# A written order for the first stages of a two-layer diffusion block on one core

## The chip, the cores and the metric

The kernel runs on one core of a Trainium2 chip. The metric is the device time of one execution in microseconds; lower is better. The core has five instruction streams that matter here: TensorE (PE, with its weight loads as PEld), VectorE (DVE), ScalarE (ACT), GpSimd (POOL) and SyncE (SP). Transfers from memory are issued from the streams of SP, ACT or POOL and carried by 16 DMA engines.

## The reference

Two layers of a transformer-like block work on 256 context tokens and 256 latent tokens of width 1024, in float32. Each layer has a token mixer (differential attention, a gated linear recurrence called HGRN, windowed attention, merged by gates) and a squared-ReLU MLP. What the change touches is the very beginning: the vectors that modulate the input, the norm of the input, and the first input projections.

```python
c_act, cc_act = silu(c), silu(c_ctx)
for l in range(DEPTH):
    m_l = split((c_act  @ w_ada[l] + b_ada[l]), 6)      # shift, scale, gate, ... latent
    m_c = split((cc_act @ w_ada[l] + b_ada[l]), 6)      # the same for the context
    h_l = rms_norm(x,   norm_g[l, 0]) * (1 + m_l[1]) + m_l[0]
    h_c = rms_norm(ctx, norm_g[l, 0]) * (1 + m_c[1]) + m_c[0]
    ... [h @ w for w in split_columns(w_in[l])] ...      # all mixers' projections
```

So the first projection needs w_ada's columns for shift and scale (1024 rows of 2048 columns) before anything can be multiplied with w_in.

## The kernel before

Float32 products are made of three matmuls on halves: a value is split into a rounded high part (`hi`, written by a ScalarE copy) and the rest (`lo`, a VectorE subtraction), and `hi*hi`, `hi*lo`, `lo*hi` are added up in PSUM (lines 248 to 250, and 260 to 262 where the activations are the stationary operand). A weight block of 1024 by 256 is loaded in two halves of 512 KB into `raw` and split into `whl` (lines 217, 226, 227); two blocks fit `whl`, a third one `arr`.

The instructions are traced in program order, and a scheduler then puts them in order on each engine by a simulation of the whole program; `high_priority` moves a piece up, and `issue_after(i)` makes an instruction stand behind `i` in its engine's queue without a wait. Temporary buffers come from an arena (`arf`, 33 units of 512 columns), the least recently freed unit first, so a load can wait for the last reader of the unit it is given. The framework gives the loads of SP's and ScalarE's queues eight semaphores in turn: one of them is issued when the load eight before it has landed.

`setup` (line 262) loads the four token tiles of 512 KB, the identity (`cst`, 64 KB), and c, c_ctx, norm_g, hgrn_lb and b_ada into two units, `ra` and `rb`. Two transposes on TensorE (lines 284, 287) make columns of them (`prm`, `bT`), and silu(c) becomes `CA`. `first_norm` normalises each token tile and transposes it (line 485) into `xT`; each 128x128 piece is copied from PSUM by itself (lines 489, 491).

`first_blocks` (line 512) then works in four groups q of 256 channels:

- sums: eight loads of w_ada, 256 KB each, as four runs of 128 columns per row, and 32 small matmuls on them (line 535, bank b7);
- vectors: the sums are copied out (line 433), transposed (line 437), and become shift and scale (lines 443, 466);
- modulation of two channel tiles of 128, k = q and 4 + q (lines 504, 506), then `hi` by ScalarE (508) and `lo` by VectorE or, for even k, GpSimd (510);
- three pieces of w_in, 256 KB each (two gate blocks and the query block of the first two HGRN heads), loaded and split (lines 546, 547).

The products with the three blocks (i = 0, 1, 2; two column halves u; banks b0 to b5; 36 matmuls of 512 columns per group, 144 in all) are traced after all four groups. Behind the last group each bank is read by a sigmoid (lines 689, 698), and the HGRN heads start on VectorE and GpSimd (lines 765, 766). `setup_mixers` then loads ten constants of the mixers (1064 KB, lines 301 to 308) on SP's queue and prepares them. The next blocks (`tm_pair`, line 260, and so on) follow.

```python
            for k in range(8):
                raw = self.A.get(1)
                load(raw[:, :].rearrange("p (j c) -> p j c", j=4),
                     wa[k * 128:k * 128 + 128, 0:2048].rearrange("p (j c) -> p j c", j=4)[:, :, qc])
```

Of the kernel before, what the change touches and what calls it, by code (L numbers as in the profile page):

```python
# [111 lines left out]
class Net:  # L112
# [152 lines left out]
    def setup(self):  # L265
# [9 lines left out]
        nc.sync.dma_start(ra[72:80, 0:128], I["c_ctx"].rearrange("(k p) -> k p", p=128))  # L275
        nc.sync.dma_start(ra[0:64, 0:128], I["norm_g"].rearrange("l i (k p) -> (l i k) p", p=128))
        nc.sync.dma_start(ra[80:96, 0:128], I["hgrn_lb"].rearrange("l r (k p) -> (l r k) p", p=128))
        nc.sync.dma_start(rb[0:96, 0:128], I["b_ada"].rearrange("l (k p) -> (l k) p", p=128))
# [19 lines left out]
    def setup_mixers(self):  # L298
        nc, A, I = self.nc, self.A, self.I
        with self.tc.issue_after(self.last_dma.ins):  # L300
            nc.sync.dma_start(self.msk, I["msk"])
            nc.sync.dma_start(self.cst[:, 128:C_END], I["cst"][:, 128:C_END])
            lv = A.get(1)
            for l in range(DEPTH):
                nc.sync.dma_start(self.sl[:, l * 128:l * 128 + 128], dram(I["diff_subln"], l * 128, [(0, 128), (1, 128)]))
                nc.sync.dma_start(self.hn[:, l * 128:l * 128 + 128], dram(I["hgrn_norm"], l * 128, [(0, 128), (1, 128)]))
                nc.sync.dma_start(self.snk[:, l * 8:l * 8 + 8], dram(I["swa_sink"], l * 8, [(0, 128), (1, 8)]))
                nc.sync.dma_start(lv[:, l * 256:l * 256 + 256], dram(I["diff_lambda"], l * 256, [(0, 128), (1, 256)]))
# [119 lines left out]
    def ada_done(self, l, g, qs=range(4), p2=None):  # L428
        nc = self.nc
        t = self.A.get(1)  # L430
        q0, nq = qs[0], len(qs)
        c = slice(q0 * 128, (q0 + nq) * 128)
        nc.vector.tensor_copy(t[:, c], self.ps[7][:, c])
        if p2 is None:
            p2 = self.mps()
        for q in qs:
            nc.tensor.transpose(p2[:, q * 128:q * 128 + 128], t[:, q * 128:q * 128 + 128], self.ident)
        t.free()
        out = self.M[l].rearrange("p (s g j q) -> p s g j q", s=2, g=3, j=4)[:, :, g]
        bb = self.bT[:, l * 48 + g * 16:l * 48 + g * 16 + 16].rearrange("p (j q) -> p j q", j=4)  # L440
        for s in range(2):
            src = view(p2, q0 * 128 + s, [(32, 4), (128, nq)])
            nc.vector.tensor_tensor(out=out[:, s, :, q0:q0 + nq], in0=src, in1=bb[:, :, q0:q0 + nq], op=ALU.add)
# [6 lines left out]
    def rstd(self, ms, cols, add=True):  # L450
# [4 lines left out]
        self.nc.gpsimd.tensor_tensor(out=r, in0=ms, in1=self.nhalf[:, 0:cols], op=ALU.pow)  # L455
        return r

    def scale_vecs(self, l, sub, q=None):

        nc = self.nc  # L460
        part = lambda t: t if q is None else t.rearrange("p (a q) -> p a q", a=2)[:, :, q]
# [9 lines left out]
    def first_norm(self):  # L471

        nc = self.nc
        xT = [self.A.get(1) for _ in range(8)]
        for tt in range(4):
# [5 lines left out]
            for b in range(2):  # L481
# [4 lines left out]
                for q in range(4):  # L486
                    c = slice(tt * 128, tt * 128 + 128)
                    if q % 2 == 0:
                        nc.scalar.copy(xT[b * 4 + q][:, c], ps[:, q * 128:q * 128 + 128])
                    else:  # L490
                        nc.vector.tensor_copy(xT[b * 4 + q][:, c], ps[:, q * 128:q * 128 + 128])
# [4 lines left out]
    def first_mod(self, xT, sv, q):  # L496
        nc = self.nc
        for k in (q, 4 + q):
            hi, lo = self.hact[k]
            for s in range(2):  # L500
                S, B = sv[s]
                x = xT[k][:, (1 - s) * LAT:(2 - s) * LAT]
                if k % 2 and s:
                    nc.scalar.activation(x, x, AF.Identity, bias=B[:, k:k + 1], scale=S[:, k:k + 1])
                else:
                    nc.vector.tensor_scalar(out=x, in0=x, scalar1=S[:, k:k + 1], scalar2=B[:, k:k + 1],
                                            op0=ALU.mult, op1=ALU.add)
            nc.scalar.copy(hi, xT[k][:, :])
            e = nc.vector if k % 2 else nc.gpsimd
            e.tensor_tensor(out=lo, in0=xT[k][:, :], in1=hi.bitcast(F32), op=ALU.subtract)  # L510
            xT[k].free()

    def first_blocks(self, offs, evacs):

# [7 lines left out]
        xT = self.first_norm()  # L522

# [4 lines left out]
        for q in range(4):  # L528
            qc = slice(q * 128, q * 128 + 128)
            for k in range(8):  # L530
                raw = self.A.get(1)
                load(raw[:, :].rearrange("p (j c) -> p j c", j=4),
                     wa[k * 128:k * 128 + 128, 0:2048].rearrange("p (j c) -> p j c", j=4)[:, :, qc])
                for j in range(4):
                    nc.tensor.matmul(self.ps[7][32 * j:32 * j + 32, qc], ca[:, k, :], raw[:, j * 128:(j + 1) * 128],
# [901 lines left out]
```

## Time and profile before

| | before |
|---|---|
| median of 3 runs | 1591.9 us (1589.07 to 1593.55) |
| the profiled execution, its own time | 1589.54 us |
| its span, first to last instruction | 1587.7 us |
| TensorE busy | 1542.0 us, 97% of the span |
| VectorE, ScalarE, GpSimd busy | 65%, 50%, 20% |
| transfers | 220.07 MB, 139 GB/s over the span |

The times of rows are counted from the span's start. TensorE is the engine that is nearly always busy; what is left to gain is where it is not, or where it runs at half its clock. A matmul row's duration includes the pipeline's drain, so the distance from one row's start to the next is the pace.

### The profile page before, as it was taken

What the parts mean: (1) busy time and instruction counts of PE and PEld (TensorE: products, weight loads), DVE (VectorE), ACT (ScalarE), POOL (GpSimd) and SP (SyncE); (2) the same over time, 40 slices, a digit from 0 to 9 for tenths busy, and PEclk for the clock granted to TensorE, in tenths of its full rate; (3) what the DMA queues carried; (4) which work ended last, traced back from release to release, by engine and by line L of the source; (5) the groups of instructions that cost most, each with busy time, mean ns of one, the idle gap of its engine ahead of it and who ended that gap; (6) DMA issues with size and microseconds to landing.
All of it is one profiled execution on the core that took longest, in us unless ns stands there. A gap on an engine that the chain in (4) does not pass through costs nothing. (4 is left out here: it accounts for less than half of the span.)

```text
span 1587.7 us, 27060 instructions
## 1 busy us (share of the span) xinstructions
PE 1542.0 (97%) x10374; PEld 1320.4 (83%) x10374; DVE 1038.5 (65%) x1938; ACT 797.7 (50%) x1646; POOL 322.8 (20%) x343
## 2 busy tenths in 40 slices
PE   6999999999999999999999999999899999989997
PEld 4788887878777778988888888999899998889996
DVE  4655634587467568887656556877758878665655
ACT  4443423356435457633424146644458776666553
POOL 1152514050330001310102011464400010221011
PEclk9999999999999999999999999999999999999999
DMA  9823234233432335575565534432434344545562
GB/s 285 238 81 120 70 119 146 70 90 101 139 93 67 109 131 184 162 225 187 172 208 190 159 100 140 132 111 77 124 99 124 94 145 109 160 133 186 186 187 92
DMA packets 209682, 220.07 MB, mean 139 GB/s; under 512 B 24400, under 2 KB 177168, under 8 KB 209552
## 3 DMA queue, kind: packets, MB, share of 16 engines
q1 hardware_dynamic: 209552, 218.34, 44.8%
q8 instruction: 81, 1.33, 0.3%
q14 instruction: 49, 0.40, 0.1%
HBM read 217.26 MB, written 1.05 MB: 137 GB/s over the span
## 5 line engine op out<-in xcount | busy, mean ns | idle before, releaser
L227 DVE TENSOR_TENSOR whl<-raw,whl 128x512 fp32r<-128x512 f32 x588 | 419.1, 732 | 248.6 <-ACT whl L226 238.7
L226 ACT CAST whl<-raw 128x512 fp32r<-128x512 f32 x588 | 355.1, 620 | 255.5 <-PE b L262 133.8
L248 PE MATMUL b<-h,whl 128*128 128x512 f32 (+1 forms) x1312 | 450.2, 345 | 2.6 <-ACT arf L938 1.4
L249 PE MATMUL b<-h,whl 128*128 128x512 f32 (+1 forms) x1312 | 446.6, 341 | 0.5 <-POOL h L606 0.4
L250 PE MATMUL b<-h,whl 128*128 128x512 f32 (+1 forms) x1312 | 446.0, 341 | 0.0
L248 PEld LDWEIGHTS b<-h,whl 128*128 128x128 f32 x1312 | 250.3, 191 | 35.5 <-ACT whl L226 2.9
L249 PEld LDWEIGHTS b<-h,whl 128*128 128x128 f32 x1312 | 249.6, 190 | 28.6 <-issue 2.5
L250 PEld LDWEIGHTS b<-h,whl 128*128 128x128 f32 x1312 | 249.2, 190 | 28.3 <-issue 2.0
L262 PE MATMUL b<-whl,arr 128*128 128x512 f32 x384 | 149.8, 390 | 0.0
L261 PE MATMUL b<-whl,arr 128*128 128x512 f32 x384 | 149.8, 390 | 0.0
L260 PE MATMUL b<-whl,arr 128*128 128x512 f32 x384 | 149.5, 390 | 0.0
L1353 POOL TENSOR_TENSOR arf<-arf 128x256 f32<-128x256 f32 (+1 forms) x70 | 61.5, 879 | 403.8 <-ACT arr L1352 346.3
L260 PE MATMUL b<-whl,h 128*128 128x256 f32 (+1 forms) x416 | 128.5, 312 | 0.7 <-DVE arf L1201 0.7
L262 PE MATMUL b<-whl,h 128*128 128x256 f32 (+1 forms) x416 | 128.3, 309 | 0.0
L261 PE MATMUL b<-whl,h 128*128 128x256 f32 (+1 forms) x416 | 128.2, 309 | 0.0
L455 POOL TENSOR_TENSOR sm<-sm,nhalf 128x1 f32<-128x1 f32 (+2 forms) x42 | 35.7, 852 | 448.9 <-DVE sm L630 244.3
L260 PEld LDWEIGHTS b<-whl,h 128*128 128x128 f32 x416 | 79.3, 191 | 7.4 <-ACT whl L226 1.3
L260 PEld LDWEIGHTS b<-whl,arr 128*128 128x128 f32 x384 | 72.1, 188 | 15.9 <-issue 1.2
L261 PEld LDWEIGHTS b<-whl,arr 128*128 128x128 f32 x384 | 72.1, 188 | 15.1 <-issue 0.4
L262 PEld LDWEIGHTS b<-whl,arr 128*128 128x128 f32 x384 | 72.1, 188 | 14.8
L809 POOL TENSOR_TENSOR arf<-arf 128x512 f32<-128x512 f32 x56 | 75.2, 1365 | 44.9 <-ACT arf L788 24.6
L261 PEld LDWEIGHTS b<-whl,h 128*128 128x128 f32 x416 | 79.3, 191 | 4.6 <-issue 0.8
(228 smaller groups left out, 2403.2 us busy)
## 6 DMA issues: line engine op xcount, KB each, us to landing
raw<-in_w_in_dram SPq DMA_DIRECT2D x110, 512.0 KB, 3.7
arf<-in_w_ada_dram SPq DMA_DIRECT2D x80, 512.0 KB, 4.8
raw<-in_w_mlp_down_dram SPq DMA_DIRECT2D x72, 512.0 KB, 3.8
raw<-in_w_mlp_up_dram SPq DMA_DIRECT2D x64, 512.0 KB, 4.5
raw<-in_w_out_dram SPq DMA_DIRECT2D x24, 512.0 KB, 3.8
arf<-in_w_ada_dram SPq DMA_DIRECT2D x32, 256.0 KB, 5.7
raw<-in_w_branch_dram SPq DMA_DIRECT2D x16, 512.0 KB, 4.0
raw<-in_w_in_dram SPq DMA_DIRECT2D x32, 128.0 KB, 2.8
```

Source lines behind the costliest of these rows:

```text
L226: self.behind(ops, lambda: nc.scalar.copy(r32(h), src))
L227: self.split_op = self.behind(ops, lambda: nc.vector.tensor_tensor(out=r32(l), in0=src, in1=h, op=ALU.subtract))
L248: nc.tensor.matmul(ps, wh, xh[:, t0:t0 + n], start=start and k == 0, stop=False)
L249: nc.tensor.matmul(ps, wh, xl[:, t0:t0 + n], start=False, stop=False)
L250: nc.tensor.matmul(ps, wl, xh[:, t0:t0 + n], start=False, stop=stop and k == nk - 1)
L260: nc.tensor.matmul(ps, xh, wh, start=start and k == 0, stop=False)
L261: nc.tensor.matmul(ps, xh, wl, start=False, stop=False)
L262: nc.tensor.matmul(ps, xl, wh, start=False, stop=stop and k == nk - 1)
L455: self.nc.gpsimd.tensor_tensor(out=r, in0=ms, in1=self.nhalf[:, 0:cols], op=ALU.pow)
L809: nc.gpsimd.tensor_tensor(out=kx, in0=kx, in1=view(cur, 1, [(nb - 1, 2), (2, nb // 2), (0, h)]), op=ALU.mult)
L1353: nc.gpsimd.tensor_tensor(out=r[:, c], in0=r[:, c], in1=r[:, c], op=ALU.mult)
```

## The change

- The four groups now hold adjacent channels: group q has the tiles k = 2q and 2q + 1. So each w_ada load has two runs of 256 columns per row in place of four of 128 (the same 256 KB), and a w_in piece is 256 adjacent rows.
- `ordered()` remembers the last instruction of TensorE, ScalarE and VectorE, and puts everything of these engines that is traced within it behind these. With it `first_blocks` writes out the whole order on the three engines: sums, copies and splits, products, vectors and modulation of the next group in between.
- The modulation writes `hi` straight from ScalarE (four activations of 256 columns for two tiles), VectorE makes the value once more and subtracts. GpSimd takes no part in it. The copies out of PSUM in `first_norm` take a whole bank each.
- The identity, c and c_ctx are loaded by GpSimd's queue, norm_g, b_ada and hgrn_lb by ScalarE's. The ten constants of the mixers go by GpSimd's queue, behind the last `pow` of `first_norm`, and are prepared behind the fourth group's modulation, ahead of the first sigmoids.
- The splits of the second weight block that follows (`set_fence(..., 1, 1)`) are queued behind the second block's sigmoids.

```diff
-        self.load_x(range(1))
-        nc.sync.dma_start(self.cst[:, 0:128], I["cst"][:, 0:128])
-        self.load_x(range(1, 4))
-        nc.sync.dma_start(ra[64:72, 0:128], I["c"].rearrange("b (k p) -> (b k) p", p=128))
...
+        nc.gpsimd.dma_start(self.cst[:, 0:128], I["cst"][:, 0:128])
+        nc.gpsimd.dma_start(ra[64:72, 0:128], I["c"].rearrange("b (k p) -> (b k) p", p=128))
+        nc.gpsimd.dma_start(ra[72:80, 0:128], I["c_ctx"].rearrange("(k p) -> k p", p=128))
+        self.load_x(range(4))
+        nc.scalar.dma_start(ra[0:64, 0:128], I["norm_g"].rearrange("l i (k p) -> (l i k) p", p=128))
+        nc.scalar.dma_start(rb[0:96, 0:128], I["b_ada"].rearrange("l (k p) -> (l k) p", p=128))
+        nc.scalar.dma_start(ra[80:96, 0:128], I["hgrn_lb"].rearrange("l r (k p) -> (l r k) p", p=128))
...
+        with self.tc.issue_after(op.ins):
             for l in range(DEPTH):
...
+                nc.gpsimd.dma_start(lv[:, l * 256:l * 256 + 256], dram(I["diff_lambda"], l * 256, [(0, 128), (1, 256)]))
+            nc.gpsimd.dma_start(self.cst[:, 128:C_END], I["cst"][:, 128:C_END])
+            nc.gpsimd.dma_start(self.msk, I["msk"])
...
+            nc.scalar.activation(hi[:, c], x, AF.Identity, bias=B[:, k:k + 1], scale=S[:, k:k + 1])
+            nc.vector.tensor_scalar(out=v[:, c], in0=x, scalar1=S[:, k:k + 1], scalar2=B[:, k:k + 1],
+                                    op0=ALU.mult, op1=ALU.add)
+        nc.vector.tensor_tensor(out=lo, in0=v[:, :], in1=hi.bitcast(F32), op=ALU.subtract)
...
+    @contextmanager
+    def ordered(self):
+
+        traced = self.nc.cur_bb.bb.instructions
+        n = len(traced)
+        with ExitStack() as st:
+            for i in self.order.values():
+                st.enter_context(self.tc.issue_after(i))
+            yield
+        for i in traced[n:]:
+            if i.engine in self.engines:
+                self.order[i.engine] = i
...
-                     wa[k * 128:k * 128 + 128, 0:2048].rearrange("p (j c) -> p j c", j=4)[:, :, qc])
...
+                load(raw[:, :].rearrange("p (s c) -> p s c", s=2),
+                     wa[k * 128:k * 128 + 128, 0:2048].rearrange("p (s q c) -> p s q c", s=2, q=4)[:, :, q])
...
+        raws, blks = loads(0)
+        lv = self.load_mixers(self.last_pow)
+        sums(0, raws, range(8))
+        t = evict(0)
+        high(0, blks, 0)
+        sv = vectors(0, t)
+        low(0, blks, 0)
+        modulation(0, sv)
+        for i in (1, 2):
+            high(0, blks, i)
+            low(0, blks, i)
         for q in range(4):
...
+            if q < 3:
+                raws, blks = loads(q + 1)
+            ks = range(8)
+            if q == 0:
+                sums(1, raws, range(2))
+                products(0, 0)
+                ks = range(2, 8)
+            if q < 3:
+                sums(q + 1, raws, ks)
+                t = evict(q + 1)
+                for i in range(n):
+                    high(q + 1, blks, i)
+                    low(q + 1, blks, i)
+            if q == 0:
+                products(0, 1)
+            else:
+                products(q, 0)
+            if q < 3:
+                modulation(q + 1, vectors(q + 1, t))
+                if q == 2:
+                    with self.ordered():
+                        self.setup_mixers(lv)
+            if q:
+                products(q, 1)
+            products(q, 2)
```

How the order moves, at three places. In these rows `b_84` to `b_89` are the banks of the products, `b_91` that of the sums, `b_90` that of the transposes of the vectors; a product's line is 248 to 250 before, 249 to 251 now.

On TensorE, from the first group's sums to the first products. Before:

```order
L535 MATMUL b_91<-arf,CA 32x128 x19
L437 MATMUL b_90<-cst,arf 128x128
L535 MATMUL b_91<-arf,CA 32x128 x16
L248 MATMUL b_84<-h,whl 128x512
L248 MATMUL b_85<-h,whl 128x512
L248 MATMUL b_86<-h,whl 128x512
L248 MATMUL b_87<-h,whl 128x512
L248 MATMUL b_88<-h,arr 128x512
L248 MATMUL b_89<-h,arr 128x512
L535 MATMUL b_91<-arf,CA 32x128 x8
```

The same place with the change:

```order
L569 MATMUL b_91<-arf,CA 32x128 x14
L583 MATMUL b_90<-cst,arf 128x128
L569 MATMUL b_91<-arf,CA 32x128 x8
L249 MATMUL b_84<-h,whl 128x512
L250 MATMUL b_84<-h,whl 128x512
L251 MATMUL b_84<-h,whl 128x512
L249 MATMUL b_85<-h,whl 128x512
L250 MATMUL b_85<-h,whl 128x512
L251 MATMUL b_85<-h,whl 128x512
```

The first products of all three blocks stood ahead of their low parts and of half of the second group's sums; now the first block's twelve products stand behind two of the second group's eight loads, and the other six loads' sums behind them.

On TensorE, the fourth group's sums and what follows them. Before, the transposition of its vectors stands here:

```order
L248 MATMUL b_89<-h,arr 128x512
L249 MATMUL b_89<-h,arr 128x512
L250 MATMUL b_89<-h,arr 128x512
L248 MATMUL b_84<-h,whl 128x512
L437 MATMUL b_90<-cst,arf 128x128
L249 MATMUL b_84<-h,whl 128x512
L250 MATMUL b_84<-h,whl 128x512
```

With the change the fourth group's sums stand in one piece, behind the second group's products:

```order
L251 MATMUL b_89<-h,arr 128x512
L569 MATMUL b_91<-arf,CA 32x128 x32
L249 MATMUL b_84<-h,whl 128x512
L250 MATMUL b_84<-h,whl 128x512
L251 MATMUL b_84<-h,whl 128x512
L249 MATMUL b_85<-h,whl 128x512
L250 MATMUL b_85<-h,whl 128x512
L251 MATMUL b_85<-h,whl 128x512
```

Before, 94 of the 144 products stand behind the fourth group's last sums; now 72 do, and the transposition (L583) stands behind the first 12 of these.

On SP's and GpSimd's queues. SP before, the last loads of `first_blocks` and what follows:

```order
L526 DMA arf<-in_w_ada_dram 128x4x128 x8
L526 DMA raw<-in_w_in_dram 128x2x256 x3
L301 DMA msk<-in_msk_dram 128x288
L302 DMA cst<-in_cst_dram 128x800
L305 DMA sl<-in_diff_subln_dram 128x128
```

SP with the change:

```order
L538 DMA arf<-in_w_ada_dram 128x2x256 x7
L218 DMA raw<-in_w_in_dram 128x4x256
L538 DMA arf<-in_w_ada_dram 128x2x256
L538 DMA raw<-in_w_in_dram 128x2x256 x3
L218 DMA raw<-in_w_in_dram 128x4x256
```

GpSimd with the change, which before has the four `pow` (line 455) here and the low parts behind them:

```order
L272 DMA cst<-in_cst_dram 128x128
L273 DMA arf<-in_c_dram 8x128
L274 DMA arf<-in_c_ctx_dram 8x128
L457 ISA
L457 TENSOR_TENSOR sm<-sm,nhalf 128x1 x4
L304 DMA arf<-in_diff_lambda_dram 128x256 x2
L305 DMA cst<-in_cst_dram 128x800
L306 DMA msk<-in_msk_dram 128x288
L308 DMA sl<-in_diff_subln_dram 128x128
```

The constants have left the place behind SP's last pieces of w_in and stand on GpSimd's queue right behind the norm; one later weight load of 512 KB has moved ahead of the last w_ada load.

## Rows read from the trace of the kernel before

**Rows 1.** The page: the span, and TensorE's busy time, share of the span, matmuls.

```profile
span 1587.7 us, 27060 instructions
PE 1542.0 (97%) x10374; PEld 1320.4 (83%) x10374; DVE 1038.5 (65%) x1938; ACT 797.7 (50%) x1646; POOL 322.8 (20%) x343
```

**Rows 2.** Windows: length, PE, PEld, DVE, ACT, POOL busy, granted clock, DMA share, GB/s.

```profile
0.00:50.00 50.00, 34.70 (x344) 24.50 (x344) 22.66 (x80) 23.63 (x49) 7.41 (x12) 0.90 1.02 289
50.00:72.00 22.00, 22.00 (x106) 17.59 (x102) 12.58 (x30) 11.87 (x22) 3.03 (x2) 1.00 0.75 231
110.00:120.00 10.00, 8.69 (x163) 6.67 (x158) 6.30 (x15) 1.81 (x3) 0.00 (x0) 1.00 0.34 107
```

**Rows 3.** Windows of the DMA stream: token tiles, then the slump, w_ada alone, weights.

```profile
6.00:8.00 2.00, 0.88 (x4) 0.88 (x5) 1.02 (x3) 0.88 (x2) 0.83 (x2) 1.00 1.00 383
8.00:14.00 6.00, 4.95 (x23) 4.29 (x22) 4.02 (x16) 5.43 (x14) 1.10 (x2) 1.00 0.83 234
32.00:34.00 2.00, 2.00 (x11) 1.64 (x10) 0.17 (x1) 0.00 (x0) 0.00 (x0) 1.00 1.17 290
62.00:64.00 2.00, 2.00 (x11) 1.65 (x10) 0.58 (x1) 0.62 (x1) 0.00 (x0) 1.00 1.09 348
```

**Rows 4.** DMA issues up to 130 us: count, KB each, us to landing.

```profile
arf<-in_w_ada_dram SPq DMA_DIRECT2D x32, 256.0 KB, 5.7
raw<-in_w_in_dram SPq DMA_DIRECT2D x12, 256.0 KB, 5.3
cst<-in_cst_dram SPq DMA_DIRECT2D x1, 400.0 KB, 5.7
...
snk<-in_swa_sink_dram SPq DMA_DIRECT2D x2, 4.0 KB, 4.2
...
arf<-in_hgrn_lb_dram SPq DMA_DIRECT2D x1, 8.0 KB, 6.4
```

**Rows 5.** Timeline of SP's queue: start, us until the next, line, tile, count.

```profile
5.73 8.14 SPq L526 DMA_DIRECT2D arf<-in_w_ada_dram  x8
```

**Rows 6.** Timeline of TensorE: start, us, line, tile, count, idle before, releaser.

```profile
10.84 0.42 PE L284 MATMUL b<-cst,arf 96*128 96x96 f32 x1 [0.90 <-DMA arf<-in_hgrn_lb_dram]
25.33 2.08 PE L248 MATMUL b<-h,whl 128*128 128x512 f32 x4
42.18 0.33 PE L437 MATMUL b<-cst,arf 128*128 128x128 f32 x1 [2.95 <-DVE arf L433]
50.03 0.50 PE L249 MATMUL b<-h,whl 128*128 128x512 f32 x1
55.18 0.27 PE L437 MATMUL b<-cst,arf 128*128 128x128 f32 x1
71.20 0.39 PE L250 MATMUL b<-h,arr 128*128 128x512 f32 x1
72.09 0.39 PE L260 MATMUL b<-whl,h 128*128 128x256 f32 x1
```

**Rows 7.** Timeline of ScalarE, VectorE and GpSimd, same columns.

```profile
48.05 1.35 ACT L546 CAST whl<-raw 128x512 fp32r<-128x512 f32 x2 [2.02 <-DMA raw<-in_w_in_dram]
58.14 1.10 ACT L504 ACTIVATE arf<-arf,M,sb 128x256 f32<-128x256 f32 x2
66.14 0.60 ACT L689 ACTIVATE arf<-b 128x512 f32<-128x512 f32 x1
...
57.59 0.73 DVE L506 TENSOR_SCALAR arf<-arf,sb,M 128x256 f32<-128x256 f32 x2
59.78 1.29 DVE L510 TENSOR_TENSOR h<-arf,h 128x512 fp32r<-128x512 f32 x2 [0.82 <-ACT h L508]
...
5.73 0.55 POOL L455 TENSOR_TENSOR sm<-sm,nhalf 128x1 f32<-128x1 f32 x1 [5.30 <-DVE sm L454]
24.02 2.50 POOL L510 TENSOR_TENSOR h<-arf,h 128x512 fp32r<-128x512 f32 x2 [12.24 <-ACT h L508]
```

**Rows 8.** Waits of TensorE from 48 to 400 us: total, times, longest.

```profile
PE b L795 <- DVE arf L812: 2.7, 4, 1.2
```

More of the change, by code (lines that the diff above doesn't have):

```diff
@@ L1 @@
 import math
-from contextlib import ExitStack, nullcontext
+from contextlib import ExitStack, contextmanager, nullcontext
+from types import SimpleNamespace
 import numpy as np
@@ L473, in first_norm @@
         nc = self.nc
-        xT = [self.A.get(1) for _ in range(8)]
+        xT = self.A.get(8)
         for tt in range(4):
@@ L522, in first_blocks @@
         xT = self.first_norm()
+        self.order = {}
+        self.engines = (nc.tensor.engine, nc.scalar.engine, nc.vector.engine)
         def load(out, src):
@@ new lines, in loads, with part, high, low @@
+                blks.append(raw)
+            return raws, blks
+        def part(q, i, o):
+            return dst[i][:, o + q * 512:o + q * 512 + 512].rearrange("p (a c) -> p a c", a=2)
+        def high(q, blks, i):
+            with self.ordered():
+                nc.scalar.copy(r32(part(q, i, 0)), blks[i])
+        def low(q, blks, i):
+            with self.ordered():
+                nc.vector.tensor_tensor(out=r32(part(q, i, 2048)), in0=blks[i], in1=part(q, i, 0), op=ALU.subtract)
+        def sums(q, raws, ks):
+            for k in ks:
+                with self.ordered():
+                    for j in range(4):
+                        nc.tensor.matmul(self.ps[7][32 * j:32 * j + 32, q * 128:q * 128 + 128], ca[:, k, :],
+                                         raws[k][:, j * 128:(j + 1) * 128], start=k == 0, stop=k == 7)
+                raws[k].free()
@@ new lines, in evict, with vectors @@
+        def evict(q):
+            t = self.A.get(1)
+            with self.ordered():
+                nc.vector.tensor_copy(t[:, 0:128], self.ps[7][:, q * 128:q * 128 + 128])
+            return t
+        def vectors(q, t):
+            p2 = self.ps[6]
+            with self.ordered():
+                nc.tensor.transpose(p2[:, q * 128:q * 128 + 128], t[:, 0:128], self.ident)
+            t.free()
+            bb = view(self.bT, 2 * q, [(8, 2), (1, 2)])
+            with self.ordered():
+                for s in range(2):
+                    nc.vector.tensor_tensor(out=view(self.M[0], s * 48 + 2 * q, [(8, 2), (1, 2)]),
+                                            in0=view(p2, q * 128 + s, [(64, 2), (32, 2)]), in1=bb, op=ALU.add)
+            with self.ordered():
+                return self.scale_vecs(0, 0, q)
@@ new lines, in modulation, with products @@
+        def modulation(q, sv):
+            for k in (2 * q, 2 * q + 1):
+                with self.ordered():
+                    self.first_mod(xT, sv, k)
+        def products(q, i):
+            hi, lo = self.w3((r32(dst[i][:, 0:2048]), r32(dst[i][:, 2048:4096])), 8)
+            for k in (2 * q, 2 * q + 1):
+                for u in range(2):
+                    with self.ordered():
+                        self.mm_cm(self.ps[i * 2 + u], (hi[:, k:k + 1], lo[:, k:k + 1]), 1, u * 128, [self.hact[k]], 0, T,
+                                   start=k == 0, stop=k == 7)
+            if q == 3:
+                with self.ordered():
+                    for u in range(2):
+                        evacs[i](u, self.ps[i * 2 + u])
+                if i == 1:
+                    self.set_fence([SimpleNamespace(ins=self.order[e]) for e in self.engines[1:]], 1, 1)
@@ L558, in first_blocks @@
         third.free()
+        xT.free()
     def prenorm(self, tt, yb):
```

102 lines of the change are left out of this document (32 added, 70 removed).

## The prediction

> **What bounds the kernel now.** I began with the page: TensorE is busy for 1542.0 of 1587.7 us [rows 1]. A change of order can only win back what TensorE idles or loses at half clock, 45.7 us of idle time at most. Windows then show where that lies. In the first 50 us TensorE is busy for 34.70, at a mean granted clock of 0.90; from 50 to 72 us it is busy throughout; in 110 to 120 it loses 1.3 us [rows 2]. So at 50 us TensorE is behind, and what counts is how much of `first_blocks` it still has to do then. Its timeline says: the fourth group's sums end just ahead of 50.03, and from there to the start of the last product at 71.20 it does 94 products and one transposition without a gap. That is 21.17 us for 93 steps, 0.228 us a product; the last is over at 71.4, and the next weight block begins at 72.09 [rows 6].
>
> Why had it done only 50 products by then? Windows of the transfers give the first reason. The 16 DMA engines are full (share 1.17), but move only 290 GB/s where w_ada alone is on its way, in runs of 512 bytes; weights in runs of 1 KB get 348, token tiles in runs of 4 KB 383 [rows 3]. The 32 loads of w_ada at 256 KB are 8.39 MB [rows 4]. The last of them lands shortly ahead of 48.05: there ScalarE's wait for the piece of w_in queued behind it ends [rows 7]. The second reason is TensorE's own order: it stood 2.95 us before 42.18 for a copy of sums on VectorE, and its first products, at 25.33, ran at half clock, four in 2.08 us [rows 6]. Their low parts were not there yet: GpSimd began on them at 24.02 and took 2.50 us for two [rows 7].
>
> **The change part by part.** I follow the last w_ada load, then what TensorE does behind it.
>
> Runs of 1 KB in place of 512 bytes: 8.39 MB at 290 GB/s are 28.9 us, at 348 GB/s 24.1. The stream gains **4.8 us**. The price of such runs is that of the weights' own loads, of the same run length.
>
> The start: from 8 to 14 us the stream runs at 234 GB/s [rows 3], and SP needs 8.14 us to issue the first eight w_ada loads [rows 5]. The fourth takes unit `ra`, and waits for the transposition on line 284, which waited for hgrn_lb until 10.84 [rows 6]; this small load, queued behind the token tiles, took 6.4 us to land [rows 4]. Now the small loads are issued at the start on two other queues, and line 284 stands behind the first tile's eight transposes. I give back the slump, 6 us times (1 - 234/290): **1.2 us**. What an issue on GpSimd's queue costs no row shows. It costs nothing as long as three take less than the 5.30 us for which GpSimd was idle before its first `pow` at 5.73 [rows 7], 1.7 us each; upward I bound it by the 6.4 us of the small load, three in a row 19 us, which is a rival below. I take nothing, since SP's issues are the nearest kind.
>
> The mixers' constants: ten loads, from the one of 400 KB to the two of 4 KB [rows 4], 1064 KB or 1.09 MB. They now go out behind the fourth `pow`, near 12 us, into a stream that is full until 48, so all that comes behind is later by 1.09 MB at 348 GB/s, **3.1 us**; nothing if they fall into gaps, 3.8 at 290. I take 3.1, since the share stands above 1. The rule for this is in the Trainium skill, DMA: Bandwidth & Descriptors, section "Issuing engines are not separate DMA queues": transfers started by any engine share the same 16 DMA engines, and a second issuer saves only the time of issuing. By the rule another queue makes no room, and the last w_ada load comes 3.1 us later; taken as if a second queue were free, the sum below would be better by these 3.1. The trace has one queue only and agrees as far as that goes, with its share of 1.17.
>
> One weight load of 512 KB now stands ahead of the last w_ada load: **1.5 us** later.
>
> Together: a piece of 256 KB takes 0.75 us, so the last w_ada load landed near 47.3 before; 47.3 - 4.8 - 1.2 + 3.1 + 1.5 = 45.9.
>
> Behind it TensorE now has the last sums (0.3, estimated from 32 in about 1 us), one transposition (0.27 [rows 6]) and 72 products, 16.4 us at 0.228: it ends at 62.9 in place of 71.4. **The gain is 8.5 us.** Two conditions. First, the other 72 products must be done by 45.9. The first can begin near 20: five us earlier than 25.33, because the first group's loads come sooner and VectorE makes the low part in 0.65 us [rows 7]. If the first twelve run at half clock (0.52 each, 6.2 us), the other 60 take 13.7 and three groups' sums 3: 22.9 of 25.9 us. Second, the fourth group's modulation must be hidden. Before, from its transposition at 55.18 to its last low part took until 59.78 + 1.29, or 5.9 us, with other splits in between [rows 6, 7]. Now 24 products stand behind the transposition, 5.5 us, and the second tile is wanted 6 products later, 6.9 us. If that cover went, TensorE would wait about 1 us. In this chain VectorE has four times 0.37 and twice 0.65, ScalarE four times 0.55 [rows 7], beside each other.
>
> At nothing go: the whole-bank copies in `first_norm` and the low parts without GpSimd (the stream, not these, sets the groups' starts); the preparation of the constants, on VectorE and ScalarE under the last 36 products, 8.2 us; and the queued splits of the second weight block, which TensorE wants a whole block later. What is late next is the first weight block's last quarter: its split waits for the second block's last product, 12 products or 2.7 us ahead of the end, and takes 0.68 on ScalarE and 0.65 on VectorE [rows 7]. That leaves 1.4 us and more.
>
> Against the profiled execution's own 1589.5 us that gives 1581.0; the median of the three runs is 2.4 us higher, and I forecast its like: 1591.9 - 8.5 = 1583.4, so **1583 us**.
>
> **The rivals.**
>
> *The constants find room.* The stream is not full around 9 to 14 us, or is quicker with several queues: 3.1 us more, 11.6 in all, **1580 us**. For it speaks the slump; against it that this slump is closed by the same change.
>
> *TensorE waits in its written order.* It now takes each group's sums in one piece, and cannot go on with products that are ready. Before, idle time was followed by the lower level of its clock, 1.2 GHz in place of 2.4: at 25.33 four products took 2.08 us [rows 6]. If twelve of the last 72 run like that, 12 times 0.29 or 3.5 us are lost: a gain of 5, **1587 us**. For it speaks that two groups' sums are waited for; against it the 3 us to spare above.
>
> *The heads give it back.* TensorE already waits for the heads' chain on VectorE, 2.7 us in four waits [rows 8], 1.3 of them between 110 and 120 [rows 2]. Before, the first sigmoid was at 66.14, 5.3 us ahead of the last product's end [rows 6, 7]. If the preparation of the constants holds the sigmoids or VectorE's part up, TensorE runs into that chain sooner: up to all of the gain, **1590 us**. Against it: the sigmoids follow the products at the same distance as before.
>
> *GpSimd's queue starts late, and it is slower.* c and c_ctx come by it now; line 284 needs them, the fourth w_ada load needs line 284, and SP's queue stands behind that load. By then SP has issued 2.1 MB of tokens and three w_ada loads, 0.79 MB: 5.5 and 2.3 us of stream, which began near 2, so it runs dry near 9.8. Each us that line 284 is later costs one. At 18.3 the gain is gone, at 23 it is slower by 0.3%; with three issues of 6.4 us each, one behind another, line 284 comes near 21 and the kernel takes **1594 us**. Against it: nothing in the trace is that slow without a full queue in front of it.
>
> **How the numbers follow.** The forecast gets 0.56, the constants' room 0.12, TensorE's waits 0.15, the heads 0.10, GpSimd's late start 0.07. A measurement of this kernel tells about 0.3%, 4.8 us, from no change: faster means under 1587.1. That is the first two cases and half of the third, 0.76; the other half and the heads are within 0.3%, 0.17; slower 0.07. The likeliest case alone spans 1579 to 1587: each price by its bounds (constants 0 to 3.8 us, slump 0 to 1.2, sums), and a later order that the scheduler shifted a little, up to 2 us either way. For 8 in 10 the range goes from 1576 to 1589; what is left out is the worse part of the heads' case, GpSimd's late start, and luck.
>
> **What the changed profile would show.** Stream: w_ada at 340 to 350 GB/s; no window below 300 between 8 and 14 us; the last small matmuls of the fourth group at 45 to 47 us. TensorE: first products near 20, then no idle time of over 1 us behind the fourth sums; the last product near 63, the second weight block's first matmul 8 to 9 us ahead of 72.09. Heads: first sigmoid near 57. Wrong would be: line 284 later than 10 us, half-clock stretches behind 45 us, or more idle time of TensorE between 95 and 115 us.

## The result: 0.7% slower

| | before | changed |
|---|---|---|
| median | 1592.12 us (4 runs) | 1602.68 us (4 runs, 1601.13 to 1603.78) |
| ratio | | 1.0074, 95% interval 1.0062 to 1.0086 |
| the profiled execution: own time, span | 1589.54, 1587.7 us | 1601.13, 1599.4 us |

I forecast 1583 us. To see where the time goes I use one measure throughout, the **lead**: the start of a TensorE matmul in the kernel before, minus the start of the same matmul (same tiles, same count) in the other kernel; the median over the matmuls that start in the 20 us from the time in the head of the column on. It comes from the profiled executions, one of each kernel. A lead that falls is time lost at that place. e1 to e12 are the experiments below.

```
start in before, us    60     140     240     340     500     580     700    1500
changed              +2.6    +0.9    +1.0    -3.2    -4.4    -8.9   -12.0   -11.3
e1_units             +5.1    +5.2    +3.7    +3.7    +3.6    +3.7    +3.7    +3.7
e2_before_units      -1.6   -10.6   -10.5   -11.9   -11.8   -16.3   -18.1   -17.3
e3_const             +8.3    +1.1    +1.1    +1.2    +1.3    +1.3    +1.3    +1.2
e9_swap              +4.0    +0.9    +1.1     0.0    -1.8    -6.7    -9.5    -8.5
e10_late             +8.3    +5.0    +5.0    +5.0    +5.3    +5.3    +5.3    +6.5
e11_runs             +1.3    +1.3    -0.2    -0.2    -0.2    -0.2    -0.2    -0.8
e12_free             -4.9    -5.0    -5.1    -5.1    -5.8    -5.8    -5.8    -4.8
```

The changed kernel does gain in its first stages, but 2.6 us, not 8.5; and then, in stages in which not one line was changed, it loses 13.9 us. First the page and the windows of the changed kernel, which answer to [rows 1, 2]:

```profile
span 1599.4 us, 27069 instructions
PE 1544.5 (97%) x10374; PEld 1323.4 (83%) x10374; DVE 1043.5 (65%) x1934; ACT 798.5 (50%) x1638; POOL 325.5 (20%) x352
```

```profile
0.00:50.00 50.00, 34.03 (x300) 25.94 (x301) 22.49 (x61) 21.15 (x37) 10.03 (x21) 0.86 0.98 312
110.00:120.00 10.00, 8.03 (x142) 7.04 (x138) 6.08 (x14) 2.27 (x4) 1.78 (x6) 1.00 0.35 105
```

TensorE's busy time in the first 50 us is no better than before. Its timeline (answering to [rows 6]) says why:

```profile
20.29 0.66 PE L569 MATMUL b<-arf,CA 128*32 128x128 f32 x8 [3.34 <-DMA arf<-in_w_ada_dram]
21.45 0.45 PE L583 MATMUL b<-cst,arf 128*128 128x128 f32 x1 [0.51 <-DVE arf L576]
26.07 1.35 PE L569 MATMUL b<-arf,CA 128*32 128x128 f32 x16 [4.18 <-DMA arf<-in_w_ada_dram]
27.35 0.80 PE L249 MATMUL b<-h,whl 128*128 128x512 f32 x1
...
50.32 1.95 PE L569 MATMUL b<-arf,CA 128*32 128x128 f32 x64
...
68.59 0.39 PE L251 MATMUL b<-h,arr 128*128 128x512 f32 x1
68.91 0.64 PE L370 MATMUL b<-arf,CA 128*32 128x256 f32 x8
69.48 0.39 PE L261 MATMUL b<-whl,h 128*128 128x256 f32 x1
```

It waits 3.34 us for the first group's last w_ada load and 4.18 for the second group's first; the first product starts at 27.35, two us later than before, not five earlier. From 26.07 it never waits again until the last product at 68.59. The fourth group's sums run in one piece, without a wait. The last w_ada load had landed at 49.1, 1.2 us before they began: issued at 42.45, it was 6.6 us under way.

```profile
42.45 0.46 SPq L538 DMA_DIRECT2D arf<-in_w_ada_dram  x1
arf<-in_w_ada_dram SPq DMA_DIRECT2D x1, 256.0 KB, 6.6
```

So this load came 3.2 us later than the 45.9 of my sum, and even so TensorE came to it later still: TensorE was the bound from 26 us on, by a small margin. The timeline of GpSimd and the transfers' rows (answering to [rows 4]) show what was in the way:

```profile
11.09 0.55 POOL L457 TENSOR_TENSOR sm<-sm,nhalf 128x1 f32<-128x1 f32 x1 [1.14 <-DMA arf<-in_w_ada_dram]
11.60 1.18 POOL L304 DMA_DIRECT2D arf<-in_diff_lambda_dram  x2
12.77 1.01 POOL L305 DMA_DIRECT2D cst<-in_cst_dram  x1
...
20.35 0.53 POOL L310 DMA_DIRECT2D snk<-in_swa_sink_dram  x1 [0.71 <-DMA arf<-in_diff_lambda_dram]
```

```profile
arf<-in_w_ada_dram SPq DMA_DIRECT2D x32, 256.0 KB, 5.9
cst<-in_cst_dram POOLq DMA_DIRECT2D x1, 400.0 KB, 10.1
arf<-in_c_ctx_dram POOLq DMA_DIRECT2D x1, 4.0 KB, 5.7
```

The constants are issued from 11.6 us on. Between 16 and 24 us the packets of the two queues took these shares of the 16 engines' time (packets, MB, share; q0 is GpSimd's queue, q1 that of SP; such shares can exceed 1 in sum, as in [rows 3]):

```profile
q1 hardware_dynamic: 1545, 1.49, 55.7%
q0 software_dynamic: 344, 0.99, 45.2%
```

The constants did not stand in line behind what SP had issued; the two queues shared the engines' time about evenly (their bytes 2 to 3), and that in the 8 us in which TensorE had little to do but wait for w_ada. The slowest w_ada load took 11.9 us to land; in the kernel before the longest that the trace shows in `first_blocks` is 6.5.

The later loss has its largest steps near 340, 540 to 580, and 660 us. At the first, VectorE's timeline of the kernel before, and then of the changed one:

```profile
335.35 0.17 DVE L1011 RECIPROCAL sm<-sm 128x2 f32<-128x2 f32 x1 [0.97 <-ACT arf L910]
335.55 0.91 DVE L1012 TENSOR_SCALAR arf<-arf,sm,lam 128x512 f32<-128x512 f32 x1
336.49 1.11 DVE L1014 SCALAR_TENSOR_TENSOR arf<-arf,sm 128x512 f32<-128x512 f32 x1
338.24 2.30 DVE L950 CAST arr<-arf 64x512 fp32r<-64x512 f32 x4 [0.64 <-POOL arf L921]
```

```profile
336.62 1.40 DVE L1041 CAST arr<-arf 64x512 fp32r<-64x512 f32 x2 [3.24 <-POOL arf L1012]
338.05 0.17 DVE L1102 RECIPROCAL sm<-sm 128x2 f32<-128x2 f32 x1
...
340.58 0.55 DVE L1103 TENSOR_SCALAR arf<-arf,sm,lam 128x512 f32<-128x512 f32 x1
...
344.33 1.21 DVE L1105 SCALAR_TENSOR_TENSOR arf<-arf,sm 128x512 f32<-128x512 f32 x1
```

The same code in another order: in the changed kernel VectorE stands 3.24 us for GpSimd with a cast, while a reciprocal, a scaling and a subtraction of the differential attention are queued behind it. TensorE needs the subtraction:

```profile
345.60 0.66 PE L1111 MATMUL b<-cst,arf 128*128 128x128 f32 x4 [3.67 <-DVE arf L1105]
```

The granted clock then falls to the lower of its levels, 1.2 GHz, for 3.4 us (0.57 of full speed on average from 346 to 350). In the kernel before this transposition started at 340.67 without a wait. Why is the order another one? Behind `first_blocks` both programs trace the same 12880 instructions. In the changed kernel 600 of them stand elsewhere in their engine's queue (387 on TensorE, 114 on VectorE, 66 on ScalarE, 24 on SP, 9 on GpSimd: the fewest that have to be moved to get from one order to the other). And what differs in their operands is the place of the buffers: the arena hands out the least recently freed unit, the rewritten `first_blocks` frees other units in another order, so every later buffer lies elsewhere.

### The profile page after: what moved, and what is told of

Its sections match the earlier page's. It is cut to its first block, busy times and chain, and to the rows that moved or that the text cites. A ratio compares the mean times of both kernels' runs of the same rounds, so it can differ in the third digit from the quotient of the medians.

```text
span 1599.4 us, 27069 instructions
## 1 busy us (share of the span) xinstructions
PE 1544.5 (97%) x10374; PEld 1323.4 (83%) x10374; DVE 1043.5 (65%) x1934; ACT 798.5 (50%) x1638; POOL 325.5 (20%) x352
## 5 line engine op out<-in xcount | busy, mean ns | idle before, releaser
L251 PEld LDWEIGHTS b<-h,whl 128*128 128x128 f32 x1312 | 249.9, 191 | 28.7 <-issue 2.0
```

The lines of the kernel that those rows point to most:

```text
L251: nc.tensor.matmul(ps, wl, xh[:, t0:t0 + n], start=False, stop=stop and k == nk - 1)
```

## The experiments

All changed lines are against the changed kernel or the experiment named; ratios are to the kernel before, with 95% intervals. The kernel before was measured again beside each experiment (medians 1590.25 to 1590.82 us, against 1592.12 beside the changed kernel), so a difference to the changed kernel is given by the ratios too.

**1, 2: units.** e1_units sets back what the arena remembers, and the two query buffers' units. e2_before_units does the reverse to the kernel before.

```diff
+UNITS = [39, 40, 45, 46, 51, 52, None, 56, 34, 35, None, None, None, None, 47, 58, 42, 53, 48, 32, 43, 54, 41, 44, 49,
+         50, None, 55, 57, 33, 36, 37, 38]
-            q = st[i]["q"] = A.get(1)
+            q = st[i]["q"] = A.get(1, (26, 6)[i] if l == 0 and hp == 0 else None)
             self.first_blocks(...)
+            A.freed = list(UNITS)
```

> The changed kernel with one thing set back: behind first_blocks the arena's record of free units (which unit was freed when) and the two units of the query buffers are those of the kernel before, so every later buffer lies in the unit it had there. First stages as changed. Theory A (the time lost behind 110 us comes from the units that later buffers get, and from the order on the engines that follows from them): the lead of 2.6 us at the first matmul of the second weight block is kept but for about 1.5 us at the heads, no wait of 3.7 us near 346 and none of 2.5 us near 579: 1589 to 1591.5 us. Rival B (it comes from the first stages' new timing itself, whatever the units): the waits near 346 and 579 stay, 1600 to 1604 us.

> The kernel before with the reverse edit: its first stages untouched, but behind them the arena's record of free units and the query buffers' units are those of the changed kernel. Theory A: it loses what the changed kernel lost behind 110 us, 10 to 14 us, with a wait of 3 to 4 us near 340 to 350: 1602 to 1606 us. Rival B: the units don't matter, 1590 to 1594 us.

e1_units took 1586.67 us, ratio 0.9977 (0.9967 to 0.9986); e2_before_units 1607.38, 1.0107 (1.0092 to 1.0122). With the units of before, 22 of the 12880 instructions stand elsewhere in place of 600; the lead stays between 3.6 and 5.2 to the end, and TensorE's waits from 340 to 350 us are down to one row:

```profile
PE b L1115 <- DVE arf L1109: 0.3, 1, 0.3
```

The reverse edit costs the old kernel 15.7 us of lead between 60 and 1500 us, more than the change's 13.9 and than my upper bound: 9.1 of it already by 140, and steps near 580 and 660 as in the changed kernel. A wait of 3 to 4 us near 345, which I expected too, is not there. Theory A holds in size, not in every place; B falls. What I had not expected is that e1_units would beat both kernels. Its first stages are the changed kernel's, but its profiled execution leads by 5.1 us at 60, that of e9_swap, again with the same first stages, by 4.0, the changed kernel's by 2.6. I read this as the spread of that start from execution to execution, not as an effect of the units; that e9_swap, with the changed kernel's own units, differs from it by 1.4, and e2_before_units, with the first stages of before, from the kernel before by 1.6, speaks for it; but no kernel was profiled twice. The parts can be read: the first product came at 27.35, 27.23 and 25.75 us (changed, e9_swap, e1_units), and from 29.0 to 32.5 the granted clock was 0.52, 0.94 and 1.00, so the first twelve products took 5.3, 4.0 and 4.3 us.

**3, 4: the loads at the start.** Both are edits of e1_units.

```diff
-        lv = self.load_mixers(self.last_pow)
...
                 raws, blks = loads(q + 1)
+                if q == 2:
+                    lv = self.load_mixers(self.last_dma)      # e3_const: nc.sync in place of nc.gpsimd
```

> e1_units with the ten loads of the mixers' constants on SP's queue behind the fourth group's last piece of w_in in place of GpSimd's queue at 11.6 us; their preparation stays where the change put it. Theory C (on GpSimd's queue they take half of the transfer engines between 16 and 24 us, while TensorE has nothing to do): the second group's first sums come near 20 in place of 26.1, first products near 20 to 22 in place of 27.35, the last product at 62 to 65 in place of 68.8, 1583.5 to 1587 us. Rival D (the stream is late for line 284 and for the order of SP's queue, the constants are hidden): first products not ahead of 25, less than 2 us better than e1_units, 1588 to 1591 us.

```diff
-        nc.gpsimd.dma_start(self.cst[:, 0:128], I["cst"][:, 0:128])
+        nc.scalar.dma_start(self.cst[:, 0:128], I["cst"][:, 0:128])    # e4_small; c and c_ctx likewise
```

> e1_units with the identity, c and c_ctx loaded by ScalarE's queue, ahead of its three, in place of GpSimd's. The fourth w_ada load was issued at 9.59 and waited for c_ctx until 8.3 and for line 284 until 9.57. Rival D: line 284 comes 1 us or more earlier, the stream's slump shrinks, 1 to 2 us better than e1_units. Theory C: the constants still come in between, TensorE's wait near 26 shrinks by less than 1 us, and ScalarE starts its norm 0.7 us later for three more issues: within 1 us of e1_units.

e3_const: 1587.44 us, 0.9985 (0.9976 to 0.9995). e4_small: 1589.31, 0.9993 (0.9983 to 1.0003). TensorE in e3_const:

```profile
19.19 0.43 PE L572 MATMUL b<-arf,CA 128*32 128x128 f32 x8 [1.75 <-DMA arf<-in_w_ada_dram]
20.30 0.50 PE L252 MATMUL b<-h,whl 128*128 128x512 f32 x1
...
61.56 0.64 PE L373 MATMUL b<-arf,CA 128*32 128x256 f32 x8
63.75 0.39 PE L264 MATMUL b<-whl,h 128*128 128x256 f32 x1 [1.55 <-ACT arf L785]
...
80.15 1.08 PE L373 MATMUL b<-arf,CA 128*32 128x256 f32 x8 [3.98 <-DMA arf<-in_w_ada_dram]
```

Theory C is right about the first stages: first product at 20.30, lead 8.3 at 60; rival D, which had the first product not ahead of 25, falls. From 16 to 24 us the stream moved 352 GB/s in e3_const, for w_ada and w_in alone, against 310 in the changed kernel with the constants among them (last column, e3_const first):

```profile
16.00:24.00 8.00, 5.21 (x35) 3.57 (x36) 5.21 (x14) 3.73 (x7) 0.00 (x0) 0.81 1.09 352
16.00:24.00 8.00, 1.53 (x17) 0.54 (x17) 2.25 (x9) 2.22 (x5) 1.47 (x3) 0.67 1.01 310
```

The time is nevertheless not better than that of e1_units, and just outside what theory C expected, for 7.2 us go again by 140: the ten small loads hold up SP's queue from 40 to 48, ScalarE waits 7.5 us for the first weights and has them at 58, its sigmoids stand behind that, and a w_ada load issued at 74 is late at 80, with half clock behind it. e4_small fits neither expectation: it is 2.6 us slower than e1_units, where D had it faster and C within 1 us. SP and ScalarE share the eight semaphores of the framework, so SP issued its first w_ada load at 4.92 us in place of 2.59, and between 10 and 18 us the stream ran at 152 GB/s against 271:

```profile
4.92 9.32 SPq L541 DMA_DIRECT2D arf<-in_w_ada_dram  x8
```

**5 to 8: the order of before, written out.** All four are e1_units with 12880 instructions each behind the one ahead of it in the kernel before; e6_const_order adds e3_const's edit, e7_swap and e8_mid their own:

```diff
-                sums(1, raws, range(2))
                 products(0, 0)
-                ks = range(2, 8)                             # e7_swap
...
+        op = nc.gpsimd.tensor_copy(out=lv[:, 0:128], in_=t[:, 0:128])    # e8_mid: t of the second group
+        with self.tc.issue_after(op.ins):
```

> e1_units, and besides the units every engine's order behind first_blocks is written out as that of the kernel before (12880 instructions, each behind the one ahead of it there). Theory A1 (with the units back, the scheduler's order is as good as that of before): within 1.5 us of e1_units, 1585 to 1588 us. Rival A2 (what is left of the order's differences costs the 1.5 us that e1_units lost near 195): 1584 to 1585.5 us.

> e3_const with the same written order behind first_blocks. In e3_const the lead of 8.3 us over the kernel before fell to 1.1 near 80, where TensorE waited 4.0 us for a later w_ada load and went to half clock; this load was issued at 74.4, behind eight weight loads, against 61.9 in e1_units. Theory E (its place in SP's queue is the cause): the load is issued before 66, no wait at 80, and 6 us or more of the lead stay at 130: 1581 to 1584.5 us. Rival F (a block that ends earlier runs into the heads' chain or into loads that are late whatever their order): the lead falls below 4 by 130, 1586 to 1589 us.

> e5_order with the first group's first twelve products ahead of the second group's first two loads' sums in TensorE's written order. In e1_units TensorE waited 4.8 us for these loads until 24.4 and began the products at 25.8. Theory G (the written order lets ready products wait): first products at 22 to 24, the last 1.5 to 3 us earlier than in e5_order, 1583 to 1585.5 us. Rival H (the low parts of the first group, or the rest of the second group's loads, end last anyway): less than 1 us.

> e5_order with the constants on GpSimd's queue behind a small copy there that reads the second group's copied sums, so that they start near 28 to 30 us in place of 11.6, and with their preparation behind the third group's modulation in place of the fourth's. Theory C: the first two groups come as early as in e3_const, the third and fourth have cover, the sigmoids wait for nothing: first products at 20 to 21, lead at 70 us 8 to 10, 1580 to 1583 us. Rival: half of the engines for the constants in the third group's time makes TensorE wait there, lead at 70 below 6, 1584 us or more.

Measured: e5_order 1595.03 us, 1.0027 (1.0016 to 1.0038); e6_const_order 1593.81, 1.0023 (1.0014 to 1.0032); e7_swap 1593.48, 1.0019 (1.0009 to 1.0028); e8_mid 1590.32, 0.9993 (0.9983 to 1.0003). A1, A2 and E fall: e5_order is 8 us slower than e1_units, which has the same units and a freer order. The waits of SP's queue between 34 and 100 us in e5_order show why:

```profile
SPq L221 <- DVE whl L231: 24.2, 5, 10.1
SPq L398 <- DVE sm L325: 12.8, 1, 12.8
```

In the order of before, a w_ada load (L398) stands ahead of three weight loads. With the new first stages its unit is one that the preparation of the constants reads late, and the weight loads stand behind it for 12.8 us. In e1_units the scheduler had put it five places further back. So an order that is right for one first stage can't be carried over to another. This costs all four kernels (that load waits 12.6 to 14.0 us in each), and of e7_swap and e8_mid I use only what happens ahead of 50 us. In e7_swap the products start at 22.23 in place of 26.88 in e5_order, but the last one at 66.69 in place of 67.04: H, the written order with its wait for the second group costs next to nothing. TensorE waits for the same loads behind the products instead, four times 0.3 us. (The medians differ by 1.5 us, which goes with the later stages and stays open.) In e8_mid the constants take the stream in the third group's time, and TensorE waits 2.85 and 2.48 us there: the rival, no room for them in the middle either. Its ten runs go from 1587.36 to 1593.33 us, and the profiled one is near the upper end.

**9: three instructions.** The changed kernel, its own units, and its own order written out but for the three instructions shown above, which stand ahead of the two casts. VectorE's order, in place of code:

```diff
-L1041 CAST x2, L1102 RECIPROCAL, ..., L1103 TENSOR_SCALAR, ..., L1105 SCALAR_TENSOR_TENSOR
+L1102 RECIPROCAL, L1103 TENSOR_SCALAR, L1105 SCALAR_TENSOR_TENSOR, L1041 CAST x2, ...
```

> The changed kernel with its own units, and with its own order behind first_blocks written out on every engine, but for three instructions: on VectorE the reciprocal, the scaling and the subtraction of one differential-attention tile (at 338.0, 340.6 and 344.3 us) stand ahead of the two casts at 336.6, as they do in the kernel before. Theory O (the units cost time by the order that the scheduler made for them): TensorE's wait of 3.7 us at 345.6 and the half clock behind it go, nothing else moves, 3.5 to 5 us better than the changed kernel: 1597.5 to 1599.5 us. Rival P (the wait there is one of buffers, whatever the order): 1601 to 1604 us.

1599.52 us, 1.0059 (1.0044 to 1.0075): 3.2 us better than the changed kernel by the medians, 2.4 by the ratios, whose intervals overlap, so the time alone does not settle it. The trace does: the lead over the changed kernel goes from 0.1 at 320 to 4.0 at 340 and is 2.6 from 350 on, TensorE's longest wait between 340 and 350 is now 0.9 us, and the granted clock stays at the upper level. Rival P falls and theory O holds at this place, with a gain below the 3.5 to 5 us that I had expected: the units cost time by way of the order. The 1.4 us by which this execution led at 60 are the spread named above, and were gone by 140. Later places I did not take apart: with the steps near 580 and 660 TensorE waits for a w_ada load (1.99 us at 577.29), and whether its unit or its place in SP's queue makes that late stays open. That the units are behind it, one way or the other, is shown by e1_units and e2_before_units.

**10: late constants on GpSimd's queue.** e1_units; the constants behind a small GpSimd copy of the fourth group's sums, prepared behind `first_blocks`, SP's queue in the order of e1_units.

> e1_units with the constants on GpSimd's queue behind a small copy there that reads the fourth group's copied sums (near 43 us), their preparation traced behind first_blocks as in the kernel before, and SP's queue in the order of e1_units. Theory C: first groups as early as in e3_const, so the lead over before is 8 us or more at 62; with SP's queue free the weights come on time, no wait for ScalarE at 64 and none for w_ada at 80: lead 6 or more at 130, 1582.5 to 1585.5 us. Rival F (TensorE runs into the heads or into the next loads): lead below 4 at 130, 1586 to 1589 us.

1585.28 us, 0.9965 (0.9953 to 0.9978), the lowest median of the study, though its interval overlaps that of e1_units. The profiled execution is the fastest of its six (1583.39). From TensorE's timeline:

```profile
21.02 1.40 PE L573 MATMUL b<-arf,CA 128*32 128x128 f32 x16 [1.74 <-DMA arf<-in_w_ada_dram]
...
62.66 0.39 PE L254 MATMUL b<-h,arr 128*128 128x512 f32 x1
...
72.29 0.39 PE L264 MATMUL b<-whl,h 128*128 128x256 f32 x1 [1.84 <-ACT arf L848]
...
78.70 0.64 PE L374 MATMUL b<-arf,CA 128*32 128x256 f32 x8 [0.41 <-DMA arf<-in_w_ada_dram]
```

Theory C again, and no clear word for F: 3.2 of the 8.3 us are lost between 60 and 80, 1.84 of them to a copy on ScalarE; 5 to 6.5 stay.

**11, 12: the other parts.** e1_units with the old channel groups (runs of 512 bytes), and e1_units without the written order.

```diff
-wa[...].rearrange("p (s q c) -> p s q c", s=2, q=4)[:, :, q]
+wa[...].rearrange("p (j q c) -> p j q c", j=4, q=4)[:, :, q]         # e11_runs; tiles q and 4 + q throughout
...
-            for i in self.order.values():
-                st.enter_context(self.tc.issue_after(i))             # e12_free
```

> e1_units with the channel groups of before again (tiles q and 4 + q), so that w_ada's loads have four runs of 512 bytes per row; all else as in e1_units. Theory R (the stream's rate counts): w_ada alone again at 290 to 295 GB/s, the second group's first sums 1 to 2 us later, the fourth group's sums 3 to 5 us later and waited for, lead at 70 us 1 to 3 in place of 5.1: 1588 to 1591 us. Rival T (TensorE is the bound from its first products on, and the stream is hidden): within 1.5 us of e1_units.

> e1_units with nothing queued by ordered(): the same instructions, their order on the three engines left to the scheduler, which again puts the first products of all three blocks ahead of half of the second group's sums. Theory W (the written order makes ready products wait): the first products at 21 to 23 in place of 25.8, last product 1 to 3 us earlier, 1584 to 1586 us. Rival X (the written order is what brings products and sums in the order in which loads land): last product 1 to 4 us later, 1587.5 to 1591 us.

e11_runs: 1590.67 us, 1.0001 (0.9992 to 1.0010), 4.0 us slower than e1_units: theory R in size, but by another path than the one expected. The first product came 2.2 us later than in e1_units (27.90), and for the fourth group's loads TensorE waited only 0.57. Its windows show the old rate (the last two columns are share and GB/s), and the same stretch of the changed kernel the new one:

```profile
36.00:40.00 4.00, 4.00 (x19) 3.25 (x18) 2.65 (x10) 1.91 (x4) 0.00 (x0) 1.00 1.16 291
```

```profile
36.00:38.00 2.00, 2.00 (x11) 1.59 (x10) 1.06 (x7) 0.37 (x1) 0.00 (x0) 1.00 1.07 349
```

e12_free: 1592.65 us, 1.0014 (1.0004 to 1.0023), 6.0 us slower than e1_units: X, and by more than I had expected, the written order is worth its while. In the profiled execution, the slowest of ten, TensorE in the scheduler's own order waits 7.18 us for the second group, ends the sums of the fourth only at 56, and is 4.9 us behind the kernel before at 60.

## Why the prediction was wrong

**The step that failed** is a half sentence near its end: "a later order that the scheduler shifted a little, up to 2 us either way". I had no row for it and took 2 us from nothing. It measured 13.9 us in the changed kernel, by its lead from 60 to 1500 us, and 16.0 between the medians of it and e1_units (15.4 by the ratios), which differ in nothing but the units and the order that follows from them. No rival held it either: my mechanism for a slower kernel was GpSimd's late start, and that did not happen (an issue there took 0.50 to 0.77 us, c_ctx landed at 8.3, line 284 ran at 9.19, within the limit of 10 that I had set).

**The second step that failed** is the bound of the first stages. I wrote "I follow the last w_ada load, then what TensorE does behind it", and charged the constants with 3.1 us at that load. They moved the first two groups, for which nothing covers, and from 26 us TensorE was the bound. The lead at 60 was 2.6, 4.0 and 5.1 in three executions of these first stages, and 8.3 in e3_const and e10_late, with the constants out of the way: 3.2 to 5.7 us, and by another mechanism. The price was too small at the last load as well: it was issued at 40.98 in e1_units and at 37.05 in e3_const, and took 7.6 and 6.7 us to land, so it came at 48.6 and 43.7, 4.9 us apart in place of 3.1:

```profile
arf<-in_w_ada_dram SPq DMA_DIRECT2D x1, 256.0 KB, 7.6
arf<-in_w_ada_dram SPq DMA_DIRECT2D x1, 256.0 KB, 6.7
```

My gain of 8.5 was nearly there at 60 us only in kernels that I did not forecast, and did not last in them. By the Trainium skill, DMA: Bandwidth & Descriptors, section "Issuing engines are not separate DMA queues", transfers started by ScalarE, SyncE or GpSimd run on the same 16 DMA engines and interleave with each other. The trace agrees: no bandwidth was won (310 GB/s against 352), and the two queues shared the engines at once; an orderly delay of all that comes behind was what I had made of it.

Point by point:

- *Runs of 1 KB*: right. 349 GB/s in place of 291, 4.0 us of time by e11_runs; I said 4.8. But half of it was lost at the first products, not at the last load.
- *The slump from 8 to 14*: wrong. It moved: 248 GB/s between 10 and 16 us, as the fourth w_ada load was issued at 9.59, behind c_ctx and line 284.
- *The fourth group's sums*: undersized. I estimated 0.3 us behind the last load; in one piece they take 1.95, and so do the third group's.
- *The weight load ahead of the last w_ada load* (1.5 us): no loss to see, for TensorE did not wait for that load.
- *Modulation hidden, splits in time*: right. From 26.07 to 68.59 there is no wait.
- *TensorE waits in its written order*: not as I priced it, for none of the last 72 products ran at half clock. There were 7.5 us of waits and twelve products at half clock (0.43 us each), but at the start, and the order was not their cause. e7_swap gains 0.35 us at the last product, e12_free loses 6.0.
- *The heads give it back*: in part, but not for the reason that I gave. Between 60 and 140 us the lead fell by 1.8, and from 62 to 150 TensorE waited 3.0 us for VectorE in the changed kernel (two rows), against 1.3 in e1_units (third row). There the first stages and the preparation of the constants are the same, and the lead stays, 5.1 and 5.2. So this loss too belongs to the units, not to the preparation:

```profile
PE b L886 <- DVE arf L903: 2.6, 4, 1.1
PE b L889 <- DVE arf L903: 0.4, 1, 0.4
PE b L890 <- DVE arf L907: 1.3, 2, 1.1
```

- *First sigmoid near 57*: it came at 65.20, 8 us later. The products ended 5.9 us later than I had summed up: the last w_ada load came 3.2 later, TensorE came to it 1.2 behind that, and the sums in one piece took 1.6 more. Loads of ScalarE's tables, the first for the constants' preparation, stand right ahead of the sigmoids, as ScalarE's timeline shows:

```profile
61.76 1.28 ACT L323 ACT_TABLE_LOAD   x1
...
63.90 1.28 ACT L781 ACT_TABLE_LOAD   x1
65.20 1.58 ACT L781 ACTIVATE arf<-b 128x512 f32<-128x512 f32 x3
```

## What to carry to other kernels

Where a scheduler or an allocator decides later stages, a change at the start is two changes: what it does there, and a new draw for all that follows. Here the draw was worth some 15 us and the edit 3.6 (e1_units against the kernel before), so test the edit with the draw held fixed (here by setting back the record of free units) before judging it. Ask of a transfer that is moved to another queue not how much it delays the end of the stream, but who waits at the moment in which it takes its share. And an order copied from another version is no safe harbour: it is right only together with the loads it was made for.

## What the runs showed of the hardware

- Two queues issued side by side shared the 16 engines: from 16 to 24 us GpSimd's took 45% of their time and SP's 56% (42 and 59 in e9_swap, 38 and 65 in e1_units). 400 KB of constants took 10.1 us to land, against 5.7 on SP's queue behind all the rest [rows 4], and w_ada loads issued beside them up to 11.9 us. Nothing was won by it: 310 GB/s, against 352 with the constants elsewhere.
- An issue on GpSimd's queue took 0.50 to 0.77 us of GpSimd at the start, less than the 1.7 that I allowed.
- The same first stages led by 2.6, 4.0 and 5.1 us in three executions: TensorE had the first group's last w_ada load at 20.3, 19.3 and 18.3 us, and the lower clock that had followed its waits ended at 32.4, 29.4 and 28.7. What made the loads differ is not shown.
